# A decoder trunk on one core: one ring of six slots for loaded weight tiles and their low parts, and other orders on ScalarE and VectorE

## The chip, the core and the metric

The kernel runs on one core of a Trainium2 chip. The metric is the time of one execution on the device in microseconds (us). Three runs of the kernel before gave 2103.29, 2104.04 and 2104.61 us, a median of 2104.04.

## The reference

A decoder of two layers runs over 256 tokens of width 2048 in float32. Layer 0 mixes with two recurrences (an RG-LRU and an HGRN2 group), layer 1 with a dilated sliding-window attention; each is followed by a squared-ReLU MLP with a hidden width of 8192. Cut to the matrix products, which are nearly all of the work:

```
h = x
for layer in range(2):
    hn  = rms_norm(h, norm_mix[layer])
    mix = recurrent(hn @ w_in) @ w_out   if layer == 0 else   attention(hn @ w_qkv) @ w_o
    h   = h + mix
    hn  = rms_norm(h, norm_mlp[layer])
    h   = h + square(relu(hn @ w1[layer])) @ w2[layer]
return rms_norm(h, final_norm)
```

All weights come from HBM in float32, each of them once or, where a combination of tiles is formed, twice. The products must hold float32 accuracy.

## The kernel before, in words

**Tiles and products.** A weight tile is 128 partitions x 2048 values, 1 MB; it holds four blocks of 128 x 512. TensorE (PE in the profile) takes a reduced form of float32, so each tile is split: ScalarE (ACT) casts it to a high part `hi`, VectorE (DVE) subtracts that from the tile and writes the rest as the low part `lo`. A product of a tile is then three matmuls per block: high by high, high weight by low activation, low weight by high activation. All splits are made by `Weights.split`.

**Units.** The list `units` fixes the order in which TensorE uses the tiles, 523 of them. The input projection (`w_in`), the gates (`w_gate`) and half of the output projection (`w_out`) use plain tiles. All other products go in 41 blocks of two token halves by two column groups (`blocks`). The first half of a block's depth is done with seven products in place of eight, on sums and differences of weight tiles and of activations; the rest with plain products. The units of a block, in the order of `ORDERS`, are:

- `t1`: the sum `s = a + t1` of two tiles; `a`: one of these alone
- `n6` or `n7`: a plain tile
- `t2`: `s` with the tile `c` added; `c`: that tile alone
- the other of `n6` and `n7`
- `t3`: tile `t1`, to which GpSimd's queue (POOL) has had a further tile added by an accumulating DMA
- `d`, `n2`, `n3`: a tile each; `t4`: `s` after a second accumulating DMA

A unit takes 12 matmuls of 128x512, a plain `n` unit 24. Seven of the blocks, in `w1`, do half of the depth's rest in the same manner and have four further, smaller units `e1` to `e4`. They are formed from the tile `e1` (in an activation buffer) and the tile `e2`, with two accumulating DMAs of 512 KB.

**Buffers.** Loaded tiles lie in a pool `wraw` of three buffers, low parts in `wlo` of three and high parts in `whi` of three, 8 KB a partition each; `t1` and `s` have one buffer each in the pool `both`. A load waits until the tile that had its raw buffer has been cast and subtracted.

**Order of the work.** `unit()` hands the next unit to TensorE and calls `fetch()`, which emits the loads, sums and splits of the unit two places ahead. Loads are issued by SyncE (SP). A scheduler orders each engine's instructions by a simulated time line and by priorities (`stream`, `urgent`). `after()` adds a pure order between two instructions of one engine. During the mixers of layer 0, ACT and DVE go in program order (`InOrder`). TensorE's order is fixed by `mm` and `turn`.

**Activations.** `to_features` turns the residual into feature-major activations (`bufa`) and forms their sums (`formx`, `formh`) for the seven products. In the attention, each of 16 heads runs four steps at places given by `PLACES` and, for the last head, `LAST_HEAD`.

The lines that place a load and its split:

```
r = wraw.tile([P, 2048], F32, name="raw")
loads[:] = [after(nc.sync.dma_start(r, src[i]), [])]
made[u] = Weights(r, 2048 if src is w_in else 1024)
```

Of the kernel before, what the change touches and what calls it, by code (L numbers as in the profile page):

```python
# [20 lines left out]
P = 128  # L21
S = 256
# [19 lines left out]
def trunk_kernel(ctx, tc, head, x, xtok, xback, cols, tab, masks, pos, fin, w_in, w_gate, w_out, w_qkv, w_o, w1, w2, out):  # L42
    nc = tc.nc
    pool = lambda name, bufs=1, **kw: ctx.enter_context(tc.tile_pool(name=name, bufs=bufs, **kw))
    cst = pool("cst")
    act = pool("act")
    wraw = pool("wraw", 3)
    whi = pool("whi", 3)
    wlo = pool("wlo", 3)
# [87 lines left out]
    at = [0, 0]  # L137

    seeds = []

    class Weights:
        def __init__(self, raw, step=2048):
            self.raw = raw
            self.hi = whi.tile([P, 2048], F32R, name="hi")
            self.lo = wlo.tile([P, 2048], F32R, name="lo")
            for at in range(0, 2048, step) if step else ():
                self.split(at, step)

        def split(self, at, n, w=None):
            h, l = self.part(at, n)  # L150
            if w is None:
                w = self.raw[:, at:at + n]
# [12 lines left out]
        def part(self, at, n):  # L165
            return self.hi[:, at:at + n], self.lo[:, at:at + n]

    def fetch():
# [4 lines left out]
        src, i = units[u][:2]  # L173
        with stream():
            if len(units[u]) > 2:
                combine(u, *units[u])
                return
            r = wraw.tile([P, 2048], F32, name="raw")
            loads[:] = [after(nc.sync.dma_start(r, src[i]), [])]
            made[u] = Weights(r, 2048 if src is w_in else 1024)  # L180

    held = {}
    turned_h = []
    first_sum = []

    def combine(u, src, i, what, i0):
        def load(name, j, home=wraw):
            held[name] = home.tile([P, 2048], F32, name="raw" if home is wraw else "bufb2" if home is act else name)
            nc.sync.dma_start(held[name], src[j])

        def add(to, x, y):
            return V.tensor_tensor(held[to], held[x], held[y], OP.add)

        if what == "t1":
            load("t1", i, both)
            load("a", i0)
# [5 lines left out]
        elif what in ("n", "d", "e2"):  # L202
            load(what, i)
        elif what == "e1":
            load("e1", i, act)
        def make(step=2048):
# [3 lines left out]
            made[u] = Weights(held[{"t1": "s", "t2": "s", "t3": "t1", "t4": "s"}.get(what, what)], step)  # L210
# [7 lines left out]
        if ahead == ("t2",):  # L218
            load("c", i0 + 5)
            nc.gpsimd.dma_start(held["t1"], src[i0 + 5], accum_op=OP.add)  # L220
            if (src is w2 and (i0 == LATE_SUM or i0 % 16 == 0)) or (src is w1 and i0 == 64):
# [1254 lines left out]
```

## Time and profile before

| | |
|---|---|
| median of three runs | 2104.04 us |
| the profiled execution | 2103.96 us |
| its span, first to last instruction | 2102.2 us |
| TensorE matmuls | 2091.9 us, 9658 instructions |
| TensorE weight loads | 1739.4 us (83%) |
| VectorE | 1765.5 us (84%) |
| ScalarE | 1394.1 us (66%) |
| GpSimd | 86.2 us (4%) |
| DMA | 509.62 MB, mean 242 GB/s |

The span is that of one profiled execution, and it lies 1.8 us under that execution's time. Line L68 is the helper through which all instructions of ScalarE and VectorE go, L302 that of the matmuls, so groups are told apart by their tiles: `hi<-raw` is the cast of a loaded tile, `lo<-raw,hi` its low part, `s<-raw,t` and `s<-s,raw` the two sums of a block. `p`, `pd`, `pt`, `po` and `pl` are banks of PSUM. In a row of the time line stand start, duration, engine, line, operation, result and operands, shape, count, and in brackets how long the engine had been idle and what ended it. `SPq` is the queue of SyncE. In the waits stand who waited for whom, total us, times and the longest.

### The profile page before, as it was taken

What the parts mean: (1) busy time and instruction counts of PE and PEld (TensorE: products, weight loads), DVE (VectorE), ACT (ScalarE), POOL (GpSimd) and SP (SyncE); (2) the same over time, 40 slices, a digit from 0 to 9 for tenths busy, and PEclk for the clock granted to TensorE, in tenths of its full rate; (3) what the DMA queues carried; (4) which work ended last, traced back from release to release, by engine and by line L of the source; (5) the groups of instructions that cost most, each with busy time, mean ns of one, the idle gap of its engine ahead of it and who ended that gap; (6) DMA issues with size and microseconds to landing.
All of it is one profiled execution on the core that took longest, in us unless ns stands there. A gap on an engine that the chain in (4) does not pass through costs nothing.

```text
span 2102.2 us, 24903 instructions
## 1 busy us (share of the span) xinstructions
PE 2091.9 (100%) x9658; PEld 1739.4 (83%) x9658; DVE 1765.5 (84%) x1688; ACT 1394.1 (66%) x1525; POOL 86.2 (4%) x105
## 2 busy tenths in 40 slices
PE   9999999999999999999999999999999999999998
PEld 8888888888888888888888888888888888888886
DVE  7686978889788889888987788799888887988887
ACT  7577556676576567467766777677755755765765
POOL 0000000000000000000000000000000000000000
PEclk9999999999999999999999999999999999999999
DMA  8544556878878878888887777778788888889785
GB/s 343 186 163 158 181 202 216 270 243 249 259 234 289 265 233 276 273 247 240 283 239 247 217 220 230 217 235 261 238 279 265 231 263 300 235 248 281 236 282 160
DMA packets 72759, 509.62 MB, mean 242 GB/s; under 512 B 8128, under 2 KB 8512, under 8 KB 12608
## 3 DMA queue, kind: packets, MB, share of 16 engines
q1 hardware_dynamic: 58320, 413.38, 52.0%
q0 software_dynamic: 14176, 94.38, 24.7%
q8 instruction: 76, 1.25, 0.2%
q14 instruction: 43, 0.35, 0.0%
q10 hardware_dynamic: 144, 0.26, 0.0%
HBM read 505.89 MB, written 2.10 MB: 242 GB/s over the span
## 4 chain that ended last, share of the span: by engine, by line
PE 96%; DVE 1%; DMA 1%; issue 1%; ACT 0%; DVEq 0%; ACTq 0%
PE p L302 60%; PE po L302 15%; PE pd L302 14%; PE pt L302 3%; PE pl L305 2%; PE pl L302 2%; DMA raw<-in_w 1%; DVE lo L68 1%; DVE s L68 0%; ACT hi L68 0%; PE po L368 0%; PE po L305 0%; DVE xall L68 0%; DVE formx L68 0%; PE pd L305 0%
## 5 line engine op out<-in xcount | busy, mean ns | idle before, releaser
L68 DVE TENSOR_TENSOR lo<-raw,hi 128x2048 fp32r<-128x2048 f32 (+2 forms) x357 | 769.0, 2161 | 136.7 <-ACT hi L68 132.5
L68 ACT CAST hi<-raw 128x2048 fp32r<-128x2048 f32 (+2 forms) x357 | 643.5, 1811 | 235.1 <-PE p L302 130.3
L302 PE MATMUL p<-hi,bufa 128*128 128x512 f32 x1888 | 477.3, 393 | 0.0
L302 PEld LDWEIGHTS p<-hi,bufa 128*128 128x128 f32 x1888 | 350.5, 188 | 70.5 <-ACT hi L68 0.2
L68 DVE TENSOR_TENSOR lo<-s,hi 128x2048 fp32r<-128x2048 f32 x123 | 281.5, 2288 | 93.9 <-ACT hi L68 93.7
L68 ACT CAST hi<-s 128x2048 fp32r<-128x2048 f32 x123 | 235.3, 1913 | 168.9 <-DVE s L68 134.1
L302 PE MATMUL p<-hi,bufb 128*128 128x512 f32 x1236 | 308.8, 390 | 0.0
L302 PEld LDWEIGHTS p<-hi,bufb 128*128 128x128 f32 x1236 | 230.8, 188 | 48.0 <-ACT hi L68 0.4
L302 PE MATMUL p<-lo,bufa 128*128 128x512 f32 x944 | 256.8, 389 | 0.0
L302 PEld LDWEIGHTS p<-lo,bufa 128*128 128x128 f32 x944 | 177.2, 188 | 37.2
L302 PE MATMUL p<-lo,bufb 128*128 128x512 f32 x618 | 167.4, 390 | 1.2 <-DVE lo L68 1.2
L302 PEld LDWEIGHTS p<-lo,bufb 128*128 128x128 f32 x618 | 115.5, 188 | 26.6 <-DVE lo L68 2.1
L68 DVE TENSOR_TENSOR s<-s,raw 128x2048 f32<-128x2048 f32 x41 | 93.7, 2285 | 5.6 <-DMA raw<-in_w_qkv 3.2
L68 DVE TENSOR_TENSOR lo<-t,hi 128x2048 fp32r<-128x2048 f32 x41 | 93.7, 2284 | 3.4 <-ACT hi L68 3.4
L68 DVE TENSOR_TENSOR s<-raw,t 128x2048 f32<-128x2048 f32 x41 | 93.7, 2284 | 0.4 <-DMA raw<-in_w 0.3
L302 PE MATMUL p<-hi,formx 128*128 128x512 f32 x368 | 92.0, 392 | 0.2 <-DVE formx L68 0.2
L68 ACT CAST hi<-t 128x2048 fp32r<-128x2048 f32 x41 | 78.6, 1917 | 18.6 <-PE po L302 7.8
L302 PE MATMUL pd<-hi,bufa 128*128 128x512 f32 x352 | 88.2, 392 | 0.0
L302 PE MATMUL po<-hi,bufb 128*128 128x512 f32 (+1 forms) x348 | 86.8, 387 | 0.0
L302 PEld LDWEIGHTS p<-hi,formx 128*128 128x128 f32 x368 | 68.5, 188 | 14.6 <-DVE formx L68 0.7
L302 PEld LDWEIGHTS pd<-hi,bufa 128*128 128x128 f32 x352 | 65.3, 188 | 13.1
L302 PE MATMUL po<-hi,bufa 128*128 128x512 f32 x292 | 76.1, 393 | 0.1
(328 smaller groups left out, 2702.0 us busy)
## 6 DMA issues: line engine op xcount, KB each, us to landing
raw<-in_w SPq DMA_DIRECT2D x217, 1024.0 KB, 6.8
raw<-in_w_in SPq DMA_DIRECT2D x45, 1024.0 KB, 4.8
raw<-in_w_qkv SPq DMA_DIRECT2D x42, 1024.0 KB, 5.1
t<-in_w SPq DMA_DIRECT2D x32, 1024.0 KB, 7.3
t<-in_w POOLq DMA_DIRECT2D x32, 1024.0 KB, 8.8
s<-in_w POOLq DMA_DIRECT2D x32, 1024.0 KB, 9.3
raw<-in_w_out SPq DMA_DIRECT2D x15, 1024.0 KB, 4.8
raw<-in_w_o SPq DMA_DIRECT2D x14, 1024.0 KB, 4.9
```

Of the source, the lines that this page charges most:

```text
L68: i = call(*args, **kw)
L302: chain[:] = [after(T.matmul(*args, **kw), chain)]
L305: chain[:] = [after(T.transpose(out_, in_, ident), chain)]
```

## The change

1. **One ring.** `wraw` and `wlo` go. An array of six slots of 8 KB a partition takes their place (`RING = 6`). Each slot can be seen as a raw tile, as a low part, or as two halves of either. The slots are given out strictly in turn (`slot`).
2. **Low part over the loaded tile.** For plain tiles, `a`, `c`, `d` and `n`, the low part is written over the loaded tile, so that the slot is held from the load until TensorE has used the low part. `t1` to `t4`, `e1`, `e2` and `e4` get a slot of their own for the low part; `e3` writes over tile `e2`. A block takes 11 slots, one with e units 13.
3. **Loads ahead.** `reserve()` emits the loads apart from the splits. `unit()` calls it, outside the input projection, for units up to five places ahead (three in `w_out`), as long as the slots it needs were last used by units that have been handed out. The loads of SP are held in program order (`queue`).
4. **Halves.** The tiles of `w_gate`, the plain ones of `w_out`, `e2` and unit 3 are loaded as two DMAs of 512 KB. The two halves of two tiles of `w1` change places on the host (`by_rows`), and the e units with them.
5. **Orders.** All casts in program order, and behind copies of `y2` and of the last head; low parts of `w_qkv` behind the last forms of `formx` made from column group 0; weight first, then the sum with `c`, in further blocks (`w_out`, the second of `w_o`, the first of `w1` in layer 0); the sum of `e2` behind the low part of the unit before; the low part of `e4` behind the subtraction of `u3`; unit 3's activations behind the casts so far. The last head's weights are turned one unit later (`LAST_HEAD`).

The matmuls and the bytes loaded are the same. The core of the diff:

```
+    nc.alloc_sbuf_tensor("arena", [P, RING * 2048], F32, side="right")
+    ring = [Slot(n) for n in range(RING)]
-    wraw = pool("wraw", 3)
-    wlo = pool("wlo", 3)
...
+    def slot(user):
+        assert users[0] < at[1]
+        users[:] = users[1:] + [user]
+        ring.append(ring.pop(0))
+        return ring[-1]
...
-            self.lo = wlo.tile([P, 2048], F32R, name="lo")
+            self.lo = lo or raw
...
-            casts[:] = [after(A.copy(h, w), seeds)]
+            casts[:] = [after(A.copy(h, w), seeds + casts)]
...
                 i = V.tensor_tensor(l, w, h.bitcast(F32), OP.subtract)
+                after(i, behind)
...
+    def needed(u):
+        what, then = ((units[v][2:3] or (None,))[0] if v < len(units) else None for v in (u, u + 1))
+        return {"t1": 2, "e2": 2, "e3": 0}.get(what, 1) + (then == "t2")
+
+    def reserve():
...
+        def load(name, j, home=None, user=u):
+            got[name] = slot(user) if home is None else home.tile([P, 2048], F32, name="bufb2" if home is act else name)
+            parts = [(got[name], slice(None))] if home else [(got[name].raw, slice(None))]
+            if name == "e2" or name == "w" and src is not w_in:
+                parts = [(got[name].raws[h], slice(1024 * h, 1024 * h + 1024)) for h in range(2)]
+            for to, cols_ in parts:
+                queue[:] = [after(nc.sync.dma_start(to, src[j][:, cols_]), queue)]
+            return queue
+
+        with stream():
+            if what is None:
+                loads[:] = load("w", i)
+            elif what == "t1":
+                load("t1", i, both)
+                load("a", i0, None, next(v for v in range(u, len(units)) if units[v][2] == "a"))
+            elif what == "e2":
+                load(what, i, None, next(v for v in range(u, len(units)) if units[v][2] == "e3"))
+            elif what in ("n", "d"):
+                load(what, i)
+            elif what == "e1":
+                load("e1", i, act)
+            if what is not None and what[0] in "te" and what != "e3":
+                got["lo"] = slot(u)
+            if u + 1 < len(units) and units[u + 1][2:3] == ("t2",):
+                load("c", i0 + 5, None, u + 2)
...
-            if (src is w2 and (i0 == LATE_SUM or i0 % 16 == 0)) or (src is w1 and i0 == 64):
+            if (src is w2 and (i0 == LATE_SUM or i0 % 16 == 0)) or src is w_out or src is w_o and i0 == 8 or (src is w1 and i0 in (0, 64)):
                 make()
                 after(add("s", "s", "c"), [made[u].ins.name])
...
-            V.tensor_tensor(sums_, sums_, raw[:, 1024:], OP.add)
-            made[u].split(1024, 1024, raw[:, 1024:])
+            raw = held["e2"].raws[0]
+            after(V.tensor_tensor(sums_, sums_, raw, OP.add), [made[u - 1].ins.name])
+            made[u].split(1024, 1024, raw)
...
         if u + 2 >= at[0]:
             fetch()
+        while (src is not w_in and at[2] < len(units) and at[2] <= u + (3 if units[at[2]][0] is w_out else 5)
+               and users[needed(at[2]) - 1] < u):
+            reserve()
...
+                if gname == 'nmix1' and not n and half:
+                    formed.append(after(i, []))
...
-                A.copy(keep["y2"], bank)
+                seeds.append(after(A.copy(keep["y2"], bank), []))
...
+                if wider(w1, i0 + 4 * n0):
+                    tc.add_manual_dep(fourth[0], after(i, []), NOSYNC, reason="order on one engine")
...
+                if hd == 15:
+                    seeds.append(after(i, []))
...
-LAST_HEAD = (4, 8, 10, 13)
+LAST_HEAD = (4, 8, 11, 13)
```

More of the change, by code (lines that the diff above doesn't have):

```diff
@@ L173, in fetch @@
         src, i = units[u][:2]
+        while at[2] <= u:
+            reserve()
+        behind[:] = formed if src is w_qkv else ()
         with stream():
+            held.update(have.pop(u))
             if len(units[u]) > 2:
@@ L177, in fetch @@
                 return
[L178 to L182, printed above, removed]
+            made[u] = Weights(held["w"], 2048 if src is w_in else 1024)
+    held, have, queue = {}, {}, []
+    def needed(u):
+        what, then = ((units[v][2:3] or (None,))[0] if v < len(units) else None for v in (u, u + 1))
+        return {"t1": 2, "e2": 2, "e3": 0}.get(what, 1) + (then == "t2")
@@ L183, in trunk_kernel @@
     turned_h = []
     first_sum = []
+    fourth = []
     def combine(u, src, i, what, i0):
[L187 to L189 removed]
         def add(to, x, y):
[L192 removed]
+            return V.tensor_tensor(*(held[n] if n in ("s", "t1") else held[n].raw for n in (to, x, y)), OP.add)
```

87 lines of the change are left out of this document (55 added, 32 removed).

## The prediction

> **What bounds the kernel now.** I read the page's first lines, then TensorE's waits, then windows over stretches of equal work, and only then single instructions. A fifth of a per cent of this kernel, 4.2 us, is about what a measurement tells from no change, so the first question is whether that much is there to be won.
>
> ```profile
> span 2102.2 us, 24903 instructions
> PE 2091.9 (100%) x9658; PEld 1739.4 (83%) x9658; DVE 1765.5 (84%) x1688; ACT 1394.1 (66%) x1525; POOL 86.2 (4%) x105
> ```
>
> TensorE (PE) is busy for 2091.9 of 2102.2 us. The 10.3 us left are mostly ends that the change doesn't touch: 1.05 us ahead of the first matmul and, after the last one (2094.05 + 0.64 = 2094.69), 7.5 us of closing norm and stores.
>
> ```profile
> 1.05 4.45 PE L368 MATMUL po<-nr 128*128 128x128 f32 x20 [1.05 <-DVE e L68]
> ...
> 2094.05 0.64 PE L302 MATMUL pt<-lo,bufb 128*128 128x256 f32 x4
> ```
>
> A busy PE can still be a slow one, so I compare stretches with the same matmuls (windows; columns: length, then busy time and count of PE, weight load, DVE, ACT, POOL, the clock, DMA share, GB/s). The first five rows are one quarter of an MLP each, two in layer 0 and three in layer 1; the last two are the start of a quarter in layer 0 and the same 568 matmuls in the kernel's last quarter.
>
> ```profile
> 577.02:742.47 165.45, 165.45 (x747) 137.32 (x747) 142.02 (x96) 107.77 (x92) 8.65 (x10) 1.00 0.83 261
> 742.47:907.90 165.43, 165.43 (x748) 137.29 (x747) 142.11 (x96) 107.43 (x92) 8.65 (x10) 1.00 0.84 261
> 1442.96:1608.50 165.54, 165.54 (x748) 137.22 (x747) 146.65 (x110) 108.50 (x95) 8.66 (x10) 1.00 0.86 263
> 1608.50:1774.13 165.63, 165.63 (x748) 137.12 (x747) 142.04 (x96) 107.35 (x92) 8.65 (x10) 1.00 0.84 260
> 1774.13:1940.22 166.09, 166.01 (x747) 137.04 (x747) 141.84 (x96) 107.26 (x92) 8.62 (x10) 1.00 0.85 260
> 742.47:867.10 124.63, 124.63 (x568) 103.51 (x567) 108.81 (x77) 85.51 (x79) 6.92 (x8) 1.00 0.82 253
> 1940.22:2067.34 127.12, 125.81 (x568) 103.18 (x567) 110.51 (x83) 87.81 (x87) 9.23 (x12) 1.00 0.83 253
> ```
>
> The clock is 1.00 everywhere. Against 165.43 the quarters of layer 1 lose 0.11, 0.20 and 0.66 us, together 0.97; the last stretch loses 127.12 - 124.63 = 2.49. One more place is the head of the qkv projection, where the first product waits for its combined activations:
>
> ```profile
> 1062.36 0.84 PE L302 MATMUL p<-hi,formx 128*128 128x512 f32 x3
> ...
> 1063.45 1.43 PE L302 MATMUL p<-hi,formx 128*128 128x512 f32 x5 [0.25 <-DVE formx L68]
> ```
>
> The first of three matmuls starts 1.09 us ahead of the fourth; at the 0.227 us of one (2.72 us for twelve) that is 0.68, so 0.41 us are lost. Sum of what can be won: 0.97 + 2.49 + 0.41 = 3.87 us. That is the ceiling for a change that leaves the matmuls and both ends alone, and it is less than 4.2.
>
> Where do the 2.49 come from? This is the chain of waits, then rows in order of time from the last quarter.
>
> ```profile
> 2023.49 12.05 DMA raw<-in_w
> ...
> 2058.42 2.21 DVE lo L68
> ```
>
> ```profile
> 2020.27 1.03 PE L305 MATMUL pl<-tab__188,y 128*128 128x128 f32 x8
> ...
> 2021.18 2.28 DVE L68 TENSOR_TENSOR lo<-raw,hi 128x2048 fp32r<-128x2048 f32 x1
> ...
> 2021.97 0.92 POOL L228 DMA_DIRECT2D s<-in_w  x1
> ...
> 2035.64 1.91 ACT L68 CAST hi<-raw 128x2048 fp32r<-128x2048 f32 x1 [7.84 <-DMA raw<-in_w]
> ...
> 2039.94 1.20 PE L302 MATMUL p<-lo,bufb 128*128 128x512 f32 x4 [0.22 <-DVE lo L68]
> ...
> 2057.67 1.98 PE L302 MATMUL p<-hi,bufb 128*128 128x512 f32 x8
> 2060.67 1.20 PE L302 MATMUL p<-lo,bufb 128*128 128x512 f32 x4 [1.02 <-DVE lo L68]
> ```
>
> The load for tile `n2` went out at 2023.49, the moment a low part that ended at 2021.18 + 2.28 = 2023.46 gave its raw buffer back, just behind POOL's accumulating load. It landed 12.05 us later, ACT stood 7.84 us, the low part came too late for PE at 2039.94, and DVE, behind from then on, was late again at 2060.67. Eight matmuls started at 2057.67 and take 1.81; PE went on after 3.00, so 1.19 us are lost there and some 1.3 around 2040. DVE sets the loads' pace: SyncE's queue (SP) waited for low parts for most of the run, and late weight loads held ACT 13 times.
>
> ```profile
> SPq L189 <- DVE lo L68: 1304.6, 259, 13.9
> ACT hi L68 <- DMA raw<-in_w: 44.0, 13, 7.8
> ```
>
> **The change, part by part.** *The ring.* Six 8 KB slots replace three raw and three low buffers, so memory is equal; what differs is who frees a slot. Before, a load waited for DVE's low part of the load three back; now it waits until PE has used the low part of the slot six back. I followed the ring through the profile's order of tiles. The block at 2009 takes slots a, t1's low, n7, c, t2's low, n6, t3's low, d, n2: n2 inherits the slot of n7, which PE leaves at 2020.27. The load goes out 2023.49 - 2020.27 = 3.2 us sooner and ahead of the accumulating load of 2021.97. ACT wanted the tile at 2035.64 - 7.84 = 2027.80, 7.5 us after the new issue. The median landing is 6.8 us:
>
> ```profile
> raw<-in_w SPq DMA_DIRECT2D x217, 1024.0 KB, 6.8
> ...
> s<-in_w POOLq DMA_DIRECT2D x32, 1024.0 KB, 9.3
> ```
>
> So all of the 7.84 goes at the median, and at worst (12.05 again) 3.2 of it, which still covers PE's 1.3 around 2040, and with it DVE's backlog at 2060.67. A load that is taken from six slots back can be held by PE alone, so what would be late next is the load that inherits the slot of a tile PE uses late; and as SP now issues in the order of the program, every later load stands behind it, with ACT's casts and DVE's sums behind those. The accumulating load of 2021.97 shares the engines with the same load as before; only which of them starts first is turned round.
>
> *The other side of the ring.* The seven blocks with the tiles e1 to e4 take 13 slots where the others take 11, and there slots come later. In the one at 1802, tile `a` gets the slot of the preceding block's t3, which PE leaves at 1783.94 + 1.07 = 1785.0; its load went out at 1780.24 before.
>
> ```profile
> 1780.24 0.33 SPq L189 DMA_DIRECT2D raw<-in_w  x1
> ...
> 1783.94 1.07 PE L302 MATMUL pd<-lo,formh 128*128 128x512 f32 x4
> ...
> 1789.48 2.29 DVE L68 TENSOR_TENSOR s<-raw,t 128x2048 f32<-128x2048 f32 x1 [0.27 <-DMA raw<-in_w]
> ...
> 1797.86 2.29 DVE L68 TENSOR_TENSOR lo<-s,hi 128x2048 fp32r<-128x2048 f32 x1 [0.69 <-ACT hi L68]
> ...
> 1800.40 1.22 DVE L68 TENSOR_TENSOR lo<-bufb,hi 128x1024 fp32r<-128x1024 f32 x1
> ...
> 1802.97 0.39 PE L302 MATMUL p<-lo,bufa 128*128 128x512 f32 x1
> ```
>
> That is 4.8 us later, with the sum `s` on DVE waiting for it at 1789.48 with nothing to spare. Behind the sum stand e1's low parts; the second ends at 1801.62, 1.35 us before PE reads it at 1802.97, and DVE has 0.69 us idle on the way. A delay of 2.0 us is therefore free and each further one is paid, seven times. From below: landing at the median 6.8 after 1785.0 is 1791.8, 2.4 late, so 0.4 a block, 2.8 in all; with fewer loads in its way (it took 9.2 us before) nothing. From above: 4.8 late costs 2.8 a block, 20 us. I take 0.1 a block, 0.7 in all, near the lower end, because the loads queued ahead of it at 1780 have 4.8 us more to drain.
>
> *Low part over the loaded tile.* A subtraction that writes over its input is in the trace: the sums do it.
>
> ```profile
> L68 DVE TENSOR_TENSOR lo<-s,hi 128x2048 fp32r<-128x2048 f32 x123 | 281.5, 2288 | 93.9 <-ACT hi L68 93.7
> ...
> L68 DVE TENSOR_TENSOR s<-s,raw 128x2048 f32<-128x2048 f32 x41 | 93.7, 2285 | 5.6 <-DMA raw<-in_w_qkv 3.2
> ```
>
> 2285 against 2288 ns: no cost either way. The number of casts, low parts and sums is unchanged.
>
> *Halved loads* (two gate tiles, eight of the output projection, seven e2, one at the start): 18 more issues of 0.33 us on SP, whose time is off PE's path; the first half arrives sooner, and e2's sum needs only that half now. Bounds: the second half later by one issue, 0.33 us, or e2's sum sooner by half a load. I take nothing.
> The Trainium skill speaks against halving: "DMA: Bandwidth & Descriptors", section Rules for kernel authors, wants 1 MiB or more per DMA, and its fit of about 2.0 us fixed plus bytes over 436 GB/s gives, as an estimate, 3.2 us for a half against 4.4 for a whole tile. If the fixed part were paid in line, a halved tile would be 2 us late; no halved load stands in this trace beside a whole one in the same stretch, and the 6.8 us of a whole one is more than the fit says.
>
> *The six orders.* All of them rank instructions on ACT and DVE. Low parts behind the last combined activation remove the 0.41 at 1063; the e2 sum behind the previous low part removes a stand of DVE; first weight, then sum, in w_out, w_o and w1's first blocks moves 2.28 us of DVE behind a low part that PE needs sooner. Casts in strict order can make a ready cast stand behind one whose sum is late, and DVE's low parts and PE behind that; ACT is idle for a third of the run, so I cost it at nothing, and without that cover at one sum, 2.28 us, in a block. Head 15's turn one unit later adds no instruction.
>
> *Sum.* Of 3.87 us I let 2.49 x 0.9 = 2.24, the 0.41 and half of 0.97 = 0.49 go, 3.14 together, and give back 0.7 at the e blocks: 2.4 us. The profiled execution took 2103.96 us, its span of 2102.2 and 1.8 around it, against a median of 2104.04, so the sum holds for the median: **2101.6 us**.
>
> **Rivals.** *No difference* (2103.5 to 2105): the ring only moves lateness about, since DMA carries the same bytes. For it: the DMA share is 0.83 in the healthy quarters too, which lose nothing. Against: the 12.05 us landing is tied to the moment of its issue. It would give 2104.0.
>
> *Slower, at the e blocks*: tile `a` late by its full 4.8 us. It decides from 2.0 us on; at 3.5 us late the price is 1.5 x 7 = 10.5, less the 3.1 won elsewhere: 2104.0 + 7.4 = 2111.4. For it: the load has no slack today, and accumulating loads of 9.3 us share the engines. Against: its 9.2 us of now are longer than the median by what stood ahead of it, and that has drained by 1785.
>
> *Faster than the ceiling*: the closing 7.5 us also shrink because ACT and DVE arrive there earlier; it needs another 0.4 us beyond all of 3.87. Little speaks for it, since that end hangs on the last matmul: 2099.6.
>
> **How the numbers follow.** Forecast 0.62 (own range 2100.2 to 2103.4), no difference 0.20, slower 0.13, faster than the ceiling 0.05. The ceiling, 2104.04 - 3.87 = 2100.17, gives the low end, rounded to 2100.0; upwards I go past no difference into the slower case, to 2107, which leaves out most of its 0.13 and the 0.05 below. Faster by over 0.2% means under 2099.8: 0.05. Slower means over 2108.25: 0.12. The rest, 0.83, is within 0.2%.
>
> **What would show it.** The load of n2 goes out near 2020 and ACT's 7.84 us shrink below 3; PE's waits for low parts at 2040 and 2060 are gone and the last stretch is back near 124.7 us; the wait for `formx` is gone; SP waits for PE rather than for low parts. In the e blocks the sum `s` waits for its load for 1 to 3 us, and e1's matmuls follow without a gap. I am wrong if a quarter of layer 0 takes longer than 165.5 us, above all by the same amount in each, or if SP's queue makes the accumulating loads so late that t2 or t4 wait.

## The result, and the profile after

The kernel after takes 2137.73 us (median; 2137.00 to 2139.43) where the kernel before takes 2103.94 (2103.03 to 2104.61): the ratio is 1.0162, with a 95% interval of 1.0149 to 1.0175. It is slower by 33.8 us; the forecast was 2101.6 with a range up to 2107.0.

The page's first lines and the largest groups of products on it (columns: count, busy us, mean ns of one, idle before), of the kernel after:

```profile
span 2135.9 us, 25187 instructions
...
PE 2126.3 (100%) x9658; PEld 1741.3 (82%) x9658; DVE 1770.9 (83%) x1688; ACT 1392.1 (65%) x1525; POOL 86.2 (4%) x105
...
L371 PE MATMUL p<-hi,bufa 128*128 128x512 f32 x1888 | 482.6, 395 | 0.5 <-ACT hi L82 0.4
...
L371 PE MATMUL p<-hi,bufb 128*128 128x512 f32 x1236 | 311.9, 393 | 0.0
...
L371 PE MATMUL p<-low,bufa 128*128 128x512 f32 x944 | 263.5, 397 | 0.6 <-DVE low L82 0.4
...
L371 PE MATMUL p<-low,bufb 128*128 128x512 f32 x618 | 171.0, 396 | 0.0
```

The same groups of the kernel before, whose program calls the low part `lo`:

```profile
L302 PE MATMUL p<-hi,bufa 128*128 128x512 f32 x1888 | 477.3, 393 | 0.0
...
L302 PE MATMUL p<-hi,bufb 128*128 128x512 f32 x1236 | 308.8, 390 | 0.0
...
L302 PE MATMUL p<-lo,bufa 128*128 128x512 f32 x944 | 256.8, 389 | 0.0
...
L302 PE MATMUL p<-lo,bufb 128*128 128x512 f32 x618 | 167.4, 390 | 1.2 <-DVE lo L68 1.2
```

PE is busy all the time, as before, and has the same 9658 products to do, but each takes longer: 6 to 8 ns more for a low part, 2 to 3 ns more for a high part. These durations overlap, so the exact account is the distance from one start to the next. Added up over all 8,678 products of 128x512 it is 1,986.6 us before and 2,020.4 after: 33.8 us, the whole difference, 3.9 ns a product. The waits are not it. What weight loads (PEld) and the load queue (SPq) waited for in the kernel after (us in total, times, longest):

```profile
PEld p L371 <- DVE low L82: 2.8, 6, 0.6
PEld p L371 <- ACT hi L82: 1.4, 2, 0.8
...
SPq L231 <- PE p L371: 877.4, 179, 11.3
SPq L231 <- PE pd L371: 300.9, 60, 8.8
SPq L231 <- DVE low L82: 289.9, 114, 8.4
```

The windows over the stretches that the prediction compared, cut at the same products (length, then busy time and count of PE, weight load, DVE, ACT, POOL, the clock, DMA share, GB/s):

```profile
586.53:755.88 169.35, 169.02 (x747) 137.22 (x747) 142.66 (x96) 107.27 (x91) 8.66 (x10) 1.00 0.82 255
755.88:924.38 168.50, 168.50 (x747) 137.30 (x747) 142.64 (x96) 107.25 (x91) 8.67 (x10) 1.00 0.83 256
1467.49:1635.98 168.49, 168.49 (x747) 137.43 (x747) 146.97 (x110) 108.06 (x94) 8.66 (x10) 1.00 0.84 258
1635.98:1804.80 168.82, 168.75 (x747) 137.31 (x747) 142.66 (x96) 107.13 (x91) 8.66 (x10) 1.00 0.82 255
1804.80:1973.38 168.58, 168.58 (x747) 137.32 (x747) 142.55 (x96) 107.20 (x91) 8.63 (x10) 1.00 0.83 256
755.88:882.78 126.90, 126.90 (x567) 103.50 (x567) 109.34 (x77) 86.28 (x79) 6.93 (x8) 1.00 0.83 257
1973.38:2100.68 127.30, 127.17 (x567) 103.52 (x567) 111.80 (x83) 88.47 (x87) 9.23 (x12) 1.00 0.84 264
```

Every quarter of an MLP is 2.5 to 3.9 us longer, in both layers, at a clock of 1.00, with PE busy throughout and the DMA share no higher than before. A loss of much the same size in every stretch that is in no wait is one of the products themselves. The prediction named this sign ("by the same amount in each") and gave it no case.

### The profile page after: what moved, and what is told of

It reads as the page before. It is cut to its first block, busy times and chain, and to the rows that moved or that the text cites. A ratio compares the mean times of both kernels' runs of the same rounds, so it can differ in the third digit from the quotient of the medians.

```text
span 2135.9 us, 25187 instructions
## 1 busy us (share of the span) xinstructions
PE 2126.3 (100%) x9658; PEld 1741.3 (82%) x9658; DVE 1770.9 (83%) x1688; ACT 1392.1 (65%) x1525; POOL 86.2 (4%) x105
## 4 chain that ended last, share of the span: by engine, by line
PE 97%; DMA 2%; DVE 1%; ACT 0%; issue 0%; ACTq 0%; DVEq 0%
PE p L371 60%; PE pd L371 15%; PE po L371 14%; PE pt L371 3%; PE pl L374 2%; DMA raw<-in_w 2%; PE pl L371 2%; DVE low L82 0%; ACT hi L82 0%; PE po L437 0%; PE po L374 0%; PE pt L374 0%; PE pd L374 0%; ACT xall L82 0%; DVE nr L82 0%
## 5 line engine op out<-in xcount | busy, mean ns | idle before, releaser
L82 DVE TENSOR_TENSOR low<-raw,hi 128x2048 fp32r<-128x2048 f32 (+2 forms) x357 | 769.9, 2161 | 134.2 <-ACT hi L82 133.2
L371 PE MATMUL p<-hi,bufa 128*128 128x512 f32 x1888 | 482.6, 395 | 0.5 <-ACT hi L82 0.4
L82 DVE TENSOR_TENSOR low<-s,hi 128x2048 fp32r<-128x2048 f32 x123 | 281.5, 2288 | 90.9 <-ACT hi L82 90.7
L371 PE MATMUL p<-low,bufa 128*128 128x512 f32 x944 | 263.5, 397 | 0.6 <-DVE low L82 0.4
L371 PEld LDWEIGHTS p<-low,bufa 128*128 128x128 f32 x944 | 176.9, 188 | 42.9 <-DVE low L82 2.8
L371 PE MATMUL p<-low,bufb 128*128 128x512 f32 x618 | 171.0, 396 | 0.0
L371 PEld LDWEIGHTS p<-low,bufb 128*128 128x128 f32 x618 | 116.0, 188 | 26.6
L82 DVE TENSOR_TENSOR low<-t,hi 128x2048 fp32r<-128x2048 f32 x41 | 93.7, 2284 | 15.0 <-ACT hi L82 15.0
L371 PEld LDWEIGHTS po<-hi,bufb 128*128 128x128 f32 x348 | 65.0, 188 | 14.9
```

The source lines that it names most:

```text
L82: i = call(*args, **kw)
L371: chain[:] = [after(T.matmul(*args, **kw), chain)]
```

## The experiments

What differs for a product is where its operands lie. The program's allocation gives each tile a start within the 128 partitions' memory, in bytes; the ring is allocated from the other end than all pools, and starts on no round number:

```
                    low parts (first)   mod 256   high parts (first)  mod 256   bufa    mod 256   formx   mod 256
before                    140288            0          115712             0     25600       0     168448      0
after                     180192          224           91136             0     25600       0     119296      0
e1_aligned                180160          192           91136             0     25600       0     119296      0
e2_low_off                140320           32          115712             0     25600       0     168512     64
e3_high_off               140352           64          115744            32     25600       0     168512     64
e5_as_before              115712            0           91136             0     25600       0     168448      0
e6, e7, e9, e11           179968            0           91136             0     25600       0     119296      0
e8_all_off                140320           32          115744            32     25632      32     168480     32
```

(A product has two operands. The stationary one, 128x128, is read by a weight load (PEld) ahead of the product; the moving one, 128x512, is read by the product itself. In this kernel `hi` and low parts, the network's weights, are the moving operands; `bufa`, `bufb`, `formx` and `formh`, the activations, hold the stationary ones, in steps of 512 bytes. `fp32r` in the rows is the reduced form of float32. In e2 and e3 what is allocated behind the low parts, `formx` and `formh`, moves by 64 bytes too.)

### First: the ring on a multiple of 64, and the kernel before off it

```
e1   -    nc.alloc_sbuf_tensor("arena", [P, RING * 2048], F32, side="right")
     +    nc.alloc_sbuf_tensor("arena", [P, RING * 2048 + 8], F32, side="right")
e2   -    wlo = pool("wlo", 3)
     +    pool("pad0").tile([P, 8], F32); wlo = pool("wlo", 3); pool("pad1").tile([P, 8], F32)
e3   the same two pads around whi instead of wlo
```

> The kernel after, its ring moved 32 bytes down so that every slot starts at a multiple of 64 bytes (180160 instead of 180192); the order of the instructions on every engine is the same. Theory A (TensorE reads a low part slower when it starts 32 bytes off a multiple of 64): the 33.8 us vanish, twelve products take 2.72 us again instead of 2.76, and the time is 2104 less what the ring wins of the predicted 2.4, so 2100 to 2104. Rival B (the cost is the additional semaphore waits ahead of weight loads, or low parts that lie where a DMA wrote): nothing changes, 2137.7. Rival C (the cost is the place of the ring high in SBUF): nothing changes either, 2137.7.

> The kernel before, its three tiles of low parts moved 32 bytes up (140320 instead of 140288); order and queues as before. Theory A: 2893 products of a low part at 10.8 ns each, 31 us, so 2133 to 2138. Rivals B and C: 2104, as no wait, no DMA and no region of the memory differs.

> The kernel before, its three tiles of high parts moved 32 bytes up, the low parts on multiples of 64 bytes. Theory A: there are twice as many products of high parts, so twice the loss, about 62 us: 2160 to 2170. Rival D (what costs is that high and low part of one tile lie differently within 64 bytes, so each switch between them costs): the same loss as with the low parts moved, 2133 to 2138. Rivals B and C: 2104.

Measured: e1 2134.44 us, ratio 1.0146 (1.0129 to 1.0163); e2 2141.76, 1.0180 (1.0165 to 1.0196); e3 2147.78, 1.0207 (1.0192 to 1.0223), against 2103.9 for the kernel before.

e2 and e3 change no instruction, no order and no transfer of the kernel before and cost it 37.9 and 43.9 us, so the addresses alone can make a loss of this size, and rivals B and C cannot be its whole cause. From their pages, e2 first:

```profile
L302 PE MATMUL p<-hi,bufa 128*128 128x512 f32 x1888 | 483.8, 396 | 0.0
...
L302 PE MATMUL p<-lo,bufa 128*128 128x512 f32 x944 | 263.2, 396 | 0.0
```

```profile
L302 PE MATMUL p<-hi,bufa 128*128 128x512 f32 x1888 | 488.4, 398 | 0.0
...
L302 PE MATMUL p<-lo,bufa 128*128 128x512 f32 x944 | 260.3, 393 | 0.0
```

In e2 the high parts, which were not moved, are slower too (393 before, 396 now). And e1 gave back 3.3 of 33.8 us: theory A was wrong in its form. 64 bytes are not the unit, and the loss doesn't go with the number of products that are moved, or e3 would have cost twice e2. Rival D predicted the same loss for e2 and e3; it fits their sizes better than A does, but not yet e1.

### Then: the addresses by themselves, and the ring where the old tiles lay

e4 computes nothing of the network. It runs cells of 24 products in the order of one tile of weights, each cell with other starts. e5 is the kernel after with

```
-    nc.alloc_sbuf_tensor("arena", [P, RING * 2048], F32, side="right")
-    base = nc.sbuf_top
+    base = 115712
...
-    whi = pool("whi", 3)
+    whi = pool("whi", 3); arena = pool("arena").tile([P, RING * 2048], F32, name="arena")
```

> Nothing of the network is computed here: 51 cells of 24 products each, in the order of a whole tile of weights (8 of the high part, 4 of the low part, twice), with nothing to wait for, and the start of the low part, of the high part or of the stationary operand moved by 4 to 2016 bytes from the place that the kernel before gives it (a remainder of 1024 by 2048). Theory A, as the first three runs leave it (the start matters, and 64 bytes aren't enough): a cell at no offset takes 24 x 226.7 ns = 5.44 us; a low part 32 bytes off costs 8 x 10.8 ns more, 5.53 us; the offset at which it falls back to 5.44 is the alignment that counts, above 64 bytes. Rival B (semaphore waits or the memory's traffic make the products slower in the kernel): every cell takes 5.44 us. Rival D (only a difference between high and low part counts): cells with both parts moved alike take 5.44.

> The kernel after with its ring at 115712 instead of 180192, so that loaded tiles, low parts and all other tiles have the remainders by 2048 that they have in the kernel before (1024 for high and low parts, 512 for formx and formh); order of the instructions as in the kernel after. Theory A: twelve products take 2.72 us again and the time is 2104 less what the ring wins, 2100 to 2104. Rival B (waits of TensorE's queue, low parts in tiles that DMAs write): 2133 to 2138, as at the two places tried so far.

Measured: e5 2106.57 us, ratio 1.0012 (1.0002 to 1.0021). With the same instructions in the same order as the kernel after, 31.2 of the 33.8 us are gone. In e4, from the first product's start to the last one's (23 distances, the first of them 0.31 us in every cell), in us, and the distance of two starts once a cell has settled:

```
low part alone moved by        0     4     8    16    32    64   128   192   256   320   384   512 to 1792 in steps of 256
24 products                  5.32  5.42  5.42  5.36  5.42  5.40  5.41  5.40  5.34  5.40  5.41  5.31 to 5.32
stationary operand alone by   16    32    64   128   256   512  1024
24 products                  5.45  5.44  5.45  5.43  5.33  5.32  5.32
high, low and stationary by   16    32    64   128   256   512  1024
24 products                  5.37  5.33  5.33  5.34  5.35  5.32  5.32
   settled, ns a product    230.0 226.7 226.7 226.7 226.7 226.7 226.7
```

This is the rule that the kernel runs into, as far as these cells go. Products run at their full pace, 226.7 ns, when their moving and their stationary operands all start at the same place within 256 bytes, wherever that is. (e10, below, shows that it isn't enough that each product's own two operands agree.) Moved together by 32 bytes they lose nothing; one of them alone, 32 bytes off, loses about 0.1 us in 24 products. The high part alone, off by 16 to 128 bytes, costs about what the low part alone does (5.37 to 5.43 us), though it has twice the products: so e3 needn't cost twice e2. (Together by 16 is an exception, at 230.0. The cells at 128 and 256 need longer to settle.) Rival B fell with e4, and D with the cells in which high and low part were moved alike and the stationary operand was not: 5.41, 5.44, 5.37 and 5.43 at 16, 32, 64 and 128 bytes.

### The rule put to the test in both kernels

e6 moves the ring to 179968, a multiple of 256 that fits (`RING * 2048 + 56`); e8 moves all of the kernel before by 32 bytes, with an 8-element pad ahead of the pool `act`; e7 is e6 with two statements of `reserve` changed over (what it is for stands below):

```
-    if what is not None and what[0] in "te" and what != "e3":
-        got["lo"] = slot(u)
     if u + 1 < len(units) and units[u + 1][2:3] == ("t2",):
         load("c", i0 + 5, None, u + 2)
+    if what is not None and what[0] in "te" and what != "e3":
+        got["lo"] = slot(u)
```

> The kernel after with its ring 224 bytes down, at 179968, a multiple of 256 but not of 512; nothing else. Theory A2 (from the probe: a product runs at full pace when the starts of its moving and its stationary operand differ by a multiple of 256 bytes): twelve products take 2.72 us and the time is that of the ring at 115712, 2105 to 2108. Rival E (the whole remainder by 512 or 2048 must be that of the kernel before, or the high end of the memory is slow): 2130 to 2138.

> The kernel before with all of its tiles for products, stationary and moving, 32 bytes up together (bufa 25632, low parts 140320). Theory A2 (only the difference of the two starts counts): no change, 2102 to 2106. Theory A as it stood first (each operand must start at a round address): more than either part alone cost, 2104 + 38 + 44 us, some 2186.

> The same, and in the seven blocks with e tiles the slot for tile c is given out, and its load issued, ahead of the slot for e2's low part, one slot sooner. Theory F (the blocks lose 0.3 to 0.9 us each because the sum s waits 2.6 us for tile c, its cast and the accumulating load behind it come late, and that load then shares the engines with n3's): the wait of s for its load, 17.3 us in seven, falls below 6, and the time is 4 to 6 us less than without it, 2100 to 2103. Rival G (thirteen slots a block are too many for six whatever their order: another tile is late next): 2105 to 2108 again.

Measured: e6 2106.28 us, ratio 1.0013 (1.0004 to 1.0022); e8 2104.45, 1.0004 (0.9995 to 1.0013). Both as theory A2 has it. Rival E fell with e6, and so did rival C, since this ring still lies at the high end of the memory. e8 has every start in the table off a multiple of 64 and is the kernel before in time, while e2, with the low parts on the very address that they have in e8, is 37 us slower: between these kernels only the difference of the starts counts. Of the 33.8 us, 31.5 are the address (2137.73 to 2106.28), and can be had back for 224 bytes.

### What is left: 2.3 to 2.7 us at the e blocks

On good addresses the change still costs 2.3 to 2.7 us where 2.4 were to be won. Windows of e6:

```profile
577.55:744.34 166.79, 166.06 (x747) 137.08 (x747) 142.56 (x96) 107.27 (x91) 8.66 (x10) 1.00 0.83 259
...
1612.17:1778.55 166.38, 165.91 (x747) 137.15 (x747) 142.55 (x96) 107.15 (x91) 8.65 (x10) 1.00 0.85 259
...
744.34:869.25 124.91, 124.91 (x567) 103.28 (x567) 109.25 (x77) 86.22 (x79) 6.91 (x8) 1.00 0.85 261
1945.06:2070.48 125.42, 125.10 (x567) 103.34 (x567) 111.60 (x83) 88.52 (x87) 9.22 (x12) 1.00 0.85 267
```

The last stretch is 1.7 us shorter than before (127.12 to 125.42); the two quarters are 1.3 and 0.8 us longer (165.45 and 165.63 before). How late the tiles of weights are used against the kernel before, from the start of their first product, in us, where it changes by more than 0.15 (e11 is told further down):

```
tile                                       before at      e6     e9    e11
v0, second tile                               10.8       0.49   0.89   0.78
w_out, block 8, tile n7                       358.7       0.53   0.79   7.52
w1 block 24 (e), its last tile t4            643.5       1.89   1.18  10.10
w1 block 40 (e), t4                          808.9       2.14   1.62  13.13
w1 block 56 (e), t4                          974.3       3.33   1.91  16.85
w_qkv, t2 of block 0                        1074.7       3.20   1.79  16.84
w_o block 0, a                              1343.8       3.25   1.88  16.88
after w1 block 72 (e): w2 64, a             1514.9       3.67   2.49  18.86
w1 block 88 (e), t4                         1675.0       4.55   3.13  21.17
w1 block 104 (e), t4                        1841.1       5.02   2.66  22.43
w1 block 120 (e), t4                        2006.7       5.62   3.31  25.15
last stretch: w2 112, t4                    2044.1       4.48   2.16  23.99
last stretch: w2 120, t2                    2064.5       3.14   0.82  22.65
```

In e6 the delay grows in the seven e blocks and almost nowhere else, by 5.1 us together, beside 0.5 at the start (there the third piece of the first input landed at 7.01 instead of 6.21 though it was issued at the same 1.65). The last stretch gives 2.5 back. The start isn't the ring's: e8, which has none, loses 0.8 us there and e9 0.9, with that piece landed sooner (5.99 and 5.87), since the first four products of 128x512 take 1.90 and 1.97 us instead of 1.17; why is open. One of these blocks, in the timeline of e6:

```profile
1816.89 2.29 DVE L82 TENSOR_TENSOR s<-s,raw 128x2048 f32<-128x2048 f32 x1 [2.57 <-DMA raw<-in_w]
...
1823.94 0.86 POOL L291 DMA_DIRECT2D s<-in_w  x1 [1.34 <-DVE low L82]
...
1837.13 1.91 ACT L82 CAST hi<-raw 128x2048 fp32r<-128x2048 f32 x1 [2.37 <-DMA raw<-in_w]
...
1841.43 1.19 PE L371 MATMUL p<-low,bufa 128*128 128x512 f32 x4 [0.22 <-DVE low L82]
```

The chain of waits of the same kernel has the transfer behind it:

```profile
1823.88 13.17 DMA raw<-in_w
```

Two loaded tiles are late. The sum `s` waits 2.57 us for tile c, and ACT 2.37 us for the block's last n. That n gets its slot at 1823.88 and starts beside POOL's accumulating load of 1823.94; both take 13 us.

e7 took up the first of the two. It measured 2116.31 us, ratio 1.0057 (1.0044 to 1.0071): slower than theory F and rival G had it, and theory F was wrong. In the block shown, c's load went out 0.2 us after the first product of e1 instead of 2.9, and landed 10.1 us later instead of 7.4, that is at the same time as ever: two halves of e2 and two accumulating loads had gone out ahead of it. DVE still stood 2.5 us. 8 of the 10 us that it lost to e6 are in one quarter and come from one place, where the planner, with c expected sooner, put c's sum ahead of two instructions that were ready:

```profile
1486.94 2.29 DVE L82 TENSOR_TENSOR s<-s,raw 128x2048 f32<-128x2048 f32 x1 [5.80 <-DMA raw<-in_w]
```

One of the two was the low part that PE needed next. PE stood 5.59 us for it, and then ran at half its clock. These are its rows, and the window over the second of them, with a clock of 0.51:

```profile
1491.49 2.07 PE L371 MATMUL p<-low,bufa 128*128 128x512 f32 x4 [5.59 <-DVE low L82]
1493.36 3.62 PE L371 MATMUL p<-hi,bufa 128*128 128x512 f32 x8
```

```profile
1493.00:1497.00 4.00, 4.00 (x11) 3.12 (x10) 3.43 (x3) 2.45 (x2) 0.88 (x1) 0.51 0.22 14
```

The twelve products from 1491.49 to 1496.78 took 5.29 us instead of 2.72. So the 8 us are 5.6 of wait and 2.6 of clock.

e9 took up the second. A slot is given out by who leaves it first, and n's and d's loads take the slots of tiles n7 and a; the orders on PE, DVE, ACT and POOL are those of e6.

```
 def slot(user):
+    order = sorted(range(RING), key=users.__getitem__)
+    users[:], ring[:] = ([l[i] for i in order] for l in (users, ring))
     assert users[0] < at[1]
-    users[:] = users[1:] + [user]
-    ring.append(ring.pop(0))
-    return ring[-1]
+    users[0] = user
+    return ring[0]
...
     elif what in ("n", "d"):
-        load(what, i)
+        hoisted(u) or load(what, i)
...
+    if what == "e3": load("d", i0 + 1, None, u + 2), load("n", i0 + 3, None, u + 4)
```

> The kernel with its ring at 179968, in which a slot is given out by who leaves it first and, in the seven blocks with e tiles, the loads of d and of the last n are given the slots that tile a and tile n7 leave; the order of the instructions on PE, DVE, ACT and POOL is unchanged. Before, that n's load went out at 1823.88 beside POOL's accumulating load (1823.94), both took 13 us, and ACT stood 2.2 us for it. Theory H (that collision costs the blocks their 0.3 to 0.9 us each): the load goes out some 3.6 us sooner, d's some 5, into the stretch in which the DMA share is 0.67; the waits of ACT for loaded tiles (17.9 us in six) fall below 8 and the time is 3 to 5 us less, 2101 to 2103.5. Rival G (the block asks for more bytes than its time gives, so whatever goes sooner makes another land later, as tile c did when its load went out 2.7 us sooner and landed no sooner): 2105 to 2108.

Measured: 2105.02 us, ratio 1.0005 (0.9996 to 1.0014). What ACT waited for loaded tiles, in e6 and then in e9:

```profile
ACT hi L82 <- DMA raw<-in_w: 17.9, 6, 3.7
```

```profile
ACT hi L82 <- DMA raw<-in_w: 7.3, 2, 3.7
```

The waits fell as theory H had it, below 8, and the time by 1.3 us where it expected 3 to 5; 2105.02 lies at the edge of rival G's range. By the table the e blocks cost 2.5 us in e9 instead of 5.1, and the start happened to be 0.3 later. The table is of one run each, and the one of e6 took 0.7 us more than its median. So what e9 changed, the collision and the sooner load of d, is between a quarter and half of the blocks' loss. The rest is not settled; the wait of the sum for tile c, 16.5 us in seven, is unchanged (16.2 in e6) and is the next candidate. e9 is the fastest of the ring's forms tried here and cannot be told from the kernel before.

e11 is e6 with the six orders undone, to see on which side they stand (the hunks of the diff on `seeds`, `casts`, `behind`, `fourth`, e2's sum, weight before sum, and `LAST_HEAD`):

```
-    casts[:] = [after(A.copy(h, w), seeds + casts)]
+    casts[:] = [after(A.copy(h, w), seeds)]
...
-    ... or src is w_out or src is w_o and i0 == 8 or (src is w1 and i0 in (0, 64)):
+    ... or (src is w1 and i0 == 64):
...
-    after(V.tensor_tensor(sums_, sums_, raw, OP.add), [made[u - 1].ins.name])
+    V.tensor_tensor(sums_, sums_, raw, OP.add)
```

> The kernel with its ring at 179968 and the six orders as the kernel before has them; the ring, its loads ahead and the halves stay. Theory L (the ring alone costs the e blocks their 5.1 us, by loads that collide, and alone wins the 2.5 us of the last stretch): matmuls after the seven e blocks stand as late as with the new orders, and the time is 2105 to 2108, up to 0.4 more for the wait of formx. Rival M (the orders cost the e blocks time, since the sum e2 is put behind a low part and casts stand in line): most of the 5.1 us go and the time is 2100 to 2103.

Measured: 2128.12 us, ratio 1.0120 (1.0104 to 1.0137), 21.8 us slower than with them. Both theories were wrong. By the table the ring without the orders loses 6.7 us at the output projection, where the chain of waits runs through a load of 6.59 us and the sum `s` of 2.29, and 1.3 to 3.7 in each e block. Of the 6.7, 2.0 us are again the clock: PE stood 1.56 and 2.25 us with one product between, the clock fell to half, and the next thirteen products took 4.94 us (360.05 to 364.99) instead of 2.95.

```profile
360.05 0.79 PE L371 MATMUL p<-hi,formh 128*128 128x512 f32 x1 [2.25 <-DVE formh L82]
```

```profile
357.00:361.00 4.00, 1.65 (x3) 1.01 (x4) 3.80 (x5) 1.35 (x5) 0.00 (x0) 0.53 0.26 109
```

What weight loads waited for in e11:

```profile
PEld p L371 <- DVE low L82: 8.2, 13, 0.8
PEld po L371 <- DVE low L82: 7.8, 7, 1.9
...
PEld p L371 <- DVE formh L82: 3.2, 2, 2.8
```

On these addresses the ring alone costs far more than the ring with the orders, which give most of that back. The six were undone together, so what each of them is worth was not measured.

### What a product's pace depends on

Two more probes asked why the starts matter.

> Nothing of the network is computed: 30 cells of 48 products each. In the first cells the starts of the moving or of the stationary operand, or of both, are moved by 32, 64 or 128 bytes in every second product, in step or in opposite step; then the stationary operand alone is moved by 16 to 256 bytes in every product. Theory J (a product is slowed by the weight load that runs beside it, which is the next product's): a cell with both moved in opposite step, so that each moving operand agrees with the stationary one of the next product, runs at 226.7 ns a product, and the cell moved in step, where each agrees with its own, is slow, 229 to 235. Rival K (a product's own two operands must agree): the other way round. Offsets of 16 to 240 bytes in every product: 229 to 235 ns; 256 bytes: 226.7.

> Nothing of the network is computed: cells of 48 products with both operands on equal starts by 256 bytes, the moving one 32, 64 or 128 bytes off, the stationary one 32 off, and both 32 off, in four kinds: fp32r with 512 moving columns as in the kernel, fp32r with 256, bf16 with 512, fp32 with 512 (16 products). Theory A2 for fp32r 512: 226.7, then 230 to 235 in the three cells with the moving operand off and the one with the stationary one off, 226.7 with both. If what counts is that two streams of reads meet, kinds that read half as many bytes in the same time (bf16) should lose less, under 3 ns a product; if it is a price per operand that isn't aligned, they lose the same 3 to 8 ns.

In e10, settled cells in which both operands are off in every second product took, at 32, 64 and 128 bytes, 233.6, 231.7 and 236.7 ns in step, and 232.5, 233.3 and 230.0 in opposite step. Neither kind is free, so J and K are both wrong: it is neither the product's own pair nor the pair with the stationary operand loaded meanwhile that has to agree. The stationary operand off in every product took 233.3 at 16, 32, 48, 64, 112, 144, 160 and 224 bytes, 228.9 to 234.4 at the others up to 208, and 226.7 at 240 and 256: 240 is a second exception. Every cell in which the starts differ from product to product is slow, also where each product's own two operands agree; by which path the two reads get in each other's way stays open.

In e12, the timeline has a row for each cell (start, us for all of its products, the product's shape). The order is: equal starts, moving operand 32, 64 and 128 bytes off, stationary one 32 off, both 32 off; then fp32r with 256 columns, equal and moving 32 off; bf16, the same two; fp32 with equal starts:

```profile
37.09 11.16 PE L49 MATMUL p<-hir,xr 128*128 128x512 f32 x48
...
48.89 11.44 PE L49 MATMUL p<-hir,xr 128*128 128x512 f32 x48
...
60.98 11.24 PE L49 MATMUL p<-hir,xr 128*128 128x512 f32 x48
...
72.86 11.39 PE L49 MATMUL p<-hir,xr 128*128 128x512 f32 x48
...
84.89 11.45 PE L49 MATMUL p<-hir,xr 128*128 128x512 f32 x48
...
96.99 11.18 PE L49 MATMUL p<-hir,xr 128*128 128x512 f32 x48
...
120.62 6.00 PE L49 MATMUL p<-hir,xr 128*128 128x256 f32 x48
...
127.28 5.86 PE L49 MATMUL p<-hir,xr 128*128 128x256 f32 x48
...
167.07 10.31 PE L49 MATMUL p<-hib,xb 128*128 128x512 bf16 x47
...
178.32 10.31 PE L49 MATMUL p<-hib,xb 128*128 128x512 bf16 x47
...
245.61 13.90 PE L49 MATMUL p<-hif,xf 128*128 128x512 f32 x32
```

fp32r with 512 columns repeats e4 (226.7 ns settled; 233.3, 228.9, 232.1, 233.3; 226.7). bf16 takes 215.8 ns in every cell, whatever the starts. An fp32 cell of 16 products has 32 records at 429.2 ns, two for each product, so a product takes 858.4 ns, in every cell too. fp32r with 256 columns takes 120.0 ns with equal starts and 116.7 to 118.7 with unequal ones, a little the other way. The loss belongs to one kind of product of the four, and it is the kind that this kernel consists of. That bf16 loses nothing goes with the guess of two streams of reads, but doesn't show it; fp32, whose operands have the same size as those of fp32r and whose products take nearly four times as long, loses nothing either.

## Why the prediction was wrong

**The ceiling** is the step that failed. It was argued "for a change that leaves the matmuls and both ends alone", and this change was taken for one, as the products' number, order and shapes stay. Their operands' addresses don't: the line that allocates the ring stood in the diff, and "memory is equal" was all that the prediction made of it. No case and no bound covered products that run slower, so the range had nothing in it above 2107. What the runs showed in its place: the ring's slots start at a remainder of 224 by 256 bytes where the activations start at 0, and each of 8,678 products is 3.9 ns longer on average; with the ring at a remainder of 0 (e6), 31.5 of the 33.8 us are gone. The step was missed, not mis-sized.

**The ring's gain** was right. On good addresses n2's load goes out at 2026.08, as soon as PE leaves the slot of n7; less the 5.6 us that e6 is late by then, that is 2020.5 (predicted 2020.27). It landed after 4.88 us instead of 12.05, ACT doesn't wait for that tile any more, and from block 120 on the table wins 2.5 us (forecast 2.24). SP waits for PE, as the rows of the kernel after show. The 0.49 us that were expected of the quarters of layer 1 didn't come: with their e blocks in them they take 165.90, 166.38 and 166.51 us in e6, 0.4 to 0.8 more than before. From the timeline of e6:

```profile
2026.08 0.33 SPq L231 DMA_DIRECT2D raw<-in_w  x1
```

**The other side of the ring**, slots that come later in the e blocks, was rightly named and seven times too small: 0.1 us a block was taken, 0.7 measured, 5.1 in all, inside the bounds of 0 and 20. That it fell between the bounds is partly luck, since the wrong tile was followed. Tile a went out 4.8 us later in the block shown, as predicted (1789.46 in e6, which is 4.4 late there), but landed after 5.2 us instead of 9.1, and its sum didn't wait; tiles c and the last n, which the thirteen slots push later as well, were not looked at.

**The six orders** were taken as worth nothing or a little. They are worth 21.8 us to this ring. The cover for that estimate, ACT idle for a third of the run, was the wrong one: by the waits of e11, what they settle is above all DVE's order between a sum and what PE needs next. The wait for `formx` is gone, and the eight products there take 1.81 us where they took 2.35. But 0.4 us were lost again within 9 us, where a low part came late (at 1074.08 in e6), so between the end of layer 0 and the qkv projection e6 wins only 0.1.

```profile
1065.73 1.98 PE L371 MATMUL p<-hi,formx 128*128 128x512 f32 x8
```

**The low part over the loaded tile and the halves** cost nothing that the runs show: the group of 357 low parts from loaded tiles takes 2161 ns in the mean in both kernels, the 123 from sums 2288 in both. On the halves, the eight plain tiles of the output projection are a direct comparison. Whole ones landed after 4.8 us in the kernel before; in the kernel after the first halves landed after 4.1 and the second, issued 0.4 later, after 5.0 (medians). So a tile's first half comes 0.7 sooner and its second 0.6 later than the whole did. By the fit of the Trainium skill ("DMA: Bandwidth & Descriptors", section Anatomy of one DMA — SWDGE (gpsimd) path), which is for DMAs issued by GpSimd where these are issued by SyncE, a whole tile would take 4.4 us and a half 3.2, as an estimate. The trace is near it for the whole, and not for the halves, which come hardly sooner; the 2 us by which a halved tile could have been late didn't show.

**The rival on the slower side** put the e blocks' price at 7.4 us, net of what is won elsewhere. With the address taken away, 2106.28 us lies between it and no difference, within the range. That would have been luck in part: the e blocks lost more and the orders did more than the sum had for them. As the sum stood, the change proper would have been 4.7 us worse than forecast.

## What to carry to other kernels

Before saying that a change leaves the products alone, compare the start addresses of the operands, and in an fp32r kernel with 512 moving columns keep all moving and stationary operands on the same remainder by 256 bytes; a tile allocated by hand from the far end doesn't get that by itself. A loss that is equal in every stretch and is in no wait is a pace, not a stall: compare mean durations of the same group before looking for releasers. And a scheme that frees buffers later should be followed for every tile that inherits one, not only for the first.

## What the runs showed of the hardware that I had not expected

A product of fp32r, 128x512, takes 226.7 ns or some 233 (up to 236.7 in a settled cell) by nothing but where its operands and those of its neighbours start within 256 bytes; the kernels here lost up to 2.1% of their time by it (e3). The Trainium skill, "SBUF — State Buffer", section "A bandwidth-pool intuition that's wrong (but worth ruling out)", gives weight loads a second, independent read port; by these runs the pace of this kind of product depends on the starts of both operands together, so in effect the two reads are not independent here, and the measurement decides; whether they meet at a port, no run shows. bf16 and fp32 products showed none of it.

A load that is issued sooner need not land sooner: tile c's in e7 went out 2.7 us earlier and was 2.7 us longer under way (10.1 instead of 7.4). It depends on what it meets: the last n's in e9, issued ahead of POOL's accumulating load and no longer beside it, landed after 5.09 us instead of 13.17.

TensorE's clock, 1.00 in all other windows shown, fell to half in the two traces in which PE stood longest in mid-kernel (5.59 us in e7; 1.56 and 2.25 in e11), and stayed there for some 7 us. The mean granted clock of every run of these two kernels is 0.997 to 0.998, that of every run of the other whole kernels here 0.999. So a wait of PE can cost more than its own length.
